# Residual and gate diagonal of the last units: from whole tiles on GpSimd to small pieces on ScalarE and VectorE

## The chip, the cores and the metric

The kernel runs on one core of one Trainium2 chip. The metric is the device time of one execution in microseconds, and the comparison is by the median of several runs. A core has a matrix engine (TensorE, PE in the profile), VectorE (DVE), ScalarE (ACT), GpSimd (POOL), and SyncE (SP), which here only issues transfers. Each engine works through its own list of instructions in the order of that list and waits for the others by semaphores.

## What is computed

One layer of a diffusion transformer on 256 tokens of 1024 channels: a token mixer, then a mixture of 64 experts (8 per token) with a shared expert, each followed by a residual sum and a LayerNorm. The change lies in the last part:

```python
x = layer_norm(alpha * x + g1 * y, ln1_g, ln1_b)
h = modulate(x, sh2, sc2)                      # normalise, scale, shift
scores = sigmoid(h @ w_router)                 # choose 8 of 64 experts per token, weights w
act = silu(einsum('td,edf->tef', h, w_e_gate)) * einsum('td,edf->tef', h, w_e_up) * gates
y2 = einsum('tef,efd->td', act, w_e_down) + shared(h)
x = layer_norm(alpha * x + g2 * y2, ln2_g, ln2_b)      # g2 from the conditioning vector
```

The change touches how `alpha * x` and the gate `g2` of the last line are prepared.

## The kernel before

The first 570 us (mixer, up to the first LayerNorm) are untouched. Then the experts are worked off in 29 units, 0 to 28. A unit is up to 128 gathered token rows of one to four experts. The weights of an expert come in two transfers of 1 MB for gate and up (`gu`) and one of 1 MB for down (`dn`), into a ring of six `gu` and seven `dn` buffers; SyncE issues each load as soon as the list in the source gives it a free buffer, and a load waits until the last matmul that reads the old content is done.

TensorE's order is written out by hand (`_program`, a list of steps, under `manual_schedule`). Per unit u: `g` gate and up (`gate_up`, line 1415, into PSUM `pgu`); `s` the first half of the scatter of unit u-1 (`scatter`, lines 1447 and 1448: matmuls into `py`, VectorE adds them to the sums `y`, which lie in `x1`); `P` the transposes of the next unit's weighted selection (`places`, `poh`, lines 1375 to 1379); `t` the activation (`act_t`: Silu on ScalarE at line 154, product with up on VectorE at line 1312, transposes `pat` on TensorE at line 1315, copy `at` on ScalarE at line 1317); `S` the second half of the scatter; on every other unit `G`, the gather of the next pair's rows (`gather`, 32 matmuls `pxg` at line 1391, evicted in turn by ScalarE, line 1394, and VectorE, line 1397); `d` the down product (line 1423), whose result is split into `rh` and `rl` (lines 1437 and 1438). `gated` (line 1365, VectorE) builds the weighted selection for the next unit. The order on ScalarE, VectorE and GpSimd comes from a scheduler that mostly follows the order of the source and the readiness of operands.

The residual of the last LayerNorm is kept as `x2h` + `x2l`, the normalised tokens in two parts, in an order of channels with k outer and p inner (channel 8p + k). `residual()` rebuilds alpha times the tokens from them, with `sd` = (alpha / rs, alpha * mu): for each of the two token tiles t, `end[:, t, :]` = (x2h + x2l) * sd0 + sd1, written to channel order, that is every eighth element for one k. It also writes `end[:, 3, :]`, the diagonal: the identity times the gate `mod2[:, 2, k]` for each k, 128x1024. `spread` (line 1534) turns this diagonal by a matmul with ones into the gate on all partitions, and ScalarE copies it into `end[:, 2, :]` (line 1535). `so_far` then multiplies the sums by the gate and adds them to the residual (lines 1542 and 1543).

`end` has no memory of its own: it takes a `gu` buffer, the first that is freed when no gate and up loads are left. That is after `gate_up` of unit 26, and the buffer is the one that held expert 5, the only expert of that unit. `spread` follows the down product of the same unit. Units 27 (experts 12 and 60) and 28 (experts 61 to 63) come after it, then `finish`, the LayerNorm and the output.

Of the kernel before, what the change touches and what calls it, by code (L numbers as in the profile page):

```python
# [9 lines left out]
F32 = mybir.dt.float32  # L10
# [3 lines left out]
AF = mybir.ActivationFunctionType  # L14
OP = mybir.AluOpType
AX = mybir.AxisListType

P = 128
D = 1024
T = 256  # L20
KD = 8
# [113 lines left out]
def build(ctx, tc, I, out, dbg=None):  # L135
    nc = tc.nc
# [31 lines left out]
    def C(name):  # L168
        a, b = _COLS[name]
        return cf[:, a:b] if b <= NKEEP else cm[:, a - NKEEP:b - NKEEP]  # L170

    ident = C("ident")
# [6 lines left out]
    mod2 = persist.tile([P, 3, KD], F32, name="mod2")  # L179
# [903 lines left out]
    for c, t, qs_ in ((0, 0, (0,)), (1, 0, (0,)), (0, 1, (0,)), (0, 0, (1,)), (1, 0, (1,)), (2, 0, (0, 1)),  # L1083
# [11 lines left out]
        if qs_[-1] == 0:  # L1095
# [4 lines left out]
                                       op0=OP.mult, op1=OP.add)  # L1100
# [43 lines left out]
    x2h = pkeep.tile([P, 2, KD, P], F32R, name="x2h")  # L1144
    x2l = pkeep.tile([P, 2, KD, P], F32R, name="x2l")
# [53 lines left out]
    for t in range(2):  # L1199
        ts = slice(t * P, (t + 1) * P)  # L1200
        for kk in (0, 4):
# [3 lines left out]
            for i in range(4):  # L1205
                k = kk + i
# [3 lines left out]
                else:  # L1210
                    on_act = nc.scalar.activation(h2[k][:, ts], pt[:, i * P:(i + 1) * P], AF.Identity,
                                                  bias=mod2[:, 0, k:k + 1], scale=mod2[:, 1, k:k + 1])
# [25 lines left out]
    for t in range(2):  # L1238
# [15 lines left out]
                                   op0=OP.add, op1=OP.mult)  # L1254
# [254 lines left out]
    def residual():  # L1509

        slot = free["g"].pop(0)
        end = ring[slot[0]].tile([P, 4, D], F32, tag=f"gu{slot[1]}", name="end", bufs=1)
        diag = end[:, 3, :].rearrange("q (k p) -> q k p", k=KD)
        nc.gpsimd.tensor_tensor(diag, ident[:, None, :].to_broadcast([P, KD, P]),
                                mod2[:, 2, :, None].to_broadcast([P, KD, P]), op=OP.mult)
        for t in range(2):
            mu, rs = stats2[t]
            sd = pkeep.tile([P, 2], F32, name=f"sd{t}")
            with tc.issue_after(last_rl[0]):
                nc.vector.reciprocal(sd[:, 0:1], rs)  # L1520
            nc.vector.tensor_scalar(sd[:, 0:1], sd[:, 0:1], ALPHA, None, op0=OP.mult)
            with tc.issue_after(last_rl[0]):
                nc.vector.tensor_scalar(sd[:, 1:2], mu, ALPHA, None, op0=OP.mult)
            e3 = end[:, t, :].rearrange("q (p k) -> q k p", k=KD)
            nc.gpsimd.tensor_tensor(e3, x2h[:, t].bitcast(F32), x2l[:, t].bitcast(F32), op=OP.add)
            nc.gpsimd.tensor_scalar(end[:, t, :], end[:, t, :], sd[:, 0:1], sd[:, 1:2], op0=OP.mult, op1=OP.add)
        return end

    def spread(end):
# [16 lines left out]
    end = None  # L1546
    assert steps[0] == ("g", 0)
    for op, i in steps[1:]:
# [8 lines left out]
        elif op == "g":  # L1557
            outs_[i] = gate_up(i)
            done("g", i)
            if end is None and free["g"] and not any(x == "g" for x, _ in loads):  # L1560
                assert i <= last_u - 2
                end, spread_at = residual(), i
        elif op == "t":
            _, used, gcol, _ = prep[i]
            ats_[i] = act_t(outs_.pop(i), gcol, used)
            if i == last_u - 1:
                so_far(end, 0)
        elif op == "d":
            if i == last_u:
                last_down(i, ats_.pop(i))  # L1570
            else:
                downs[i] = down(i, ats_.pop(i))
            if end is not None and i == spread_at:
                spread(end)
            done("d", i)
        else:
            n = "sS".index(op)
            (scatter_open if i == last_u - 1 else scatter)(n, *downs[i])
            if n and i == last_u - 2:
                so_far(end, 1)  # L1580
                xf, g2bc = end[:, 0:2, :], end[:, 2, :]
# [31 lines left out]
    with tc.If(nov > 0):  # L1613
# [3 lines left out]
        for k in range(KD):  # L1617
            px = ps_mm("px")
            for t in range(2):
                for part in (x2h, x2l):  # L1620
# [3 lines left out]
                                    op0=OP.mult, op1=OP.add)  # L1624
# [52 lines left out]
```

## Time and profile before

| | us |
|---|---|
| median of 3 runs (1095.12 to 1095.26) | 1095.15 |
| the profiled execution | 1096.06 |
| its span, first to last instruction | 1094.2 |
| TensorE busy | 1046.6 (96%) |
| VectorE busy | 636.2 (58%) |
| ScalarE busy | 424.1 (39%) |
| GpSimd busy | 91.1 (8%) |
| mean granted TensorE clock | 0.991 |

A busy TensorE is not TensorE at its peak: matmuls are pipelined, so that the durations of neighbours overlap, and the start of the next one tells more than the duration. [...] Timeline rows merge neighbours of one kind, and a bracket at a row's end is the engine's idle time before it and what ended it by the profile. Where an instruction waits for several semaphores, the one that came last is named, which can be a coincidence.

### The profile page before, as it was taken

The page shows a single profiled execution, that of the slowest core. Times are in us where ns is not written, and L with a number is a line of the kernel's source. Part 1 is how long each engine was busy: PE and PEld are TensorE (multiplying, and loading weights), DVE is VectorE, ACT ScalarE, POOL GpSimd, SP SyncE. Part 2 cuts the span into 40 slices and gives each one's busy share as a digit, 9 for nine tenths or more (in the row PEclk, how much of TensorE's full clock was granted, in tenths as well). Part 3 has the DMA queues.
Part 4 walks back from the last instruction along what each step waited for, and adds up shares of the span by engine and source line. Part 5 has one row for each costly group of instructions (what it writes and reads, how often), then busy time and mean ns, then how long its engine had stood idle before and what let it go on. Part 6 is the DMA issues. An engine that isn't in the chain of part 4 may idle for free.

```text
span 1094.2 us, 19256 instructions
## 1 busy us (share of the span) xinstructions
PE 1046.6 (96%) x7488; PEld 727.3 (66%) x7488; DVE 636.2 (58%) x1339; ACT 424.1 (39%) x779; POOL 91.1 (8%) x135
## 2 busy tenths in 40 slices
PE   4999999999999999999999899999999999999994
PEld 3797877979899988889997444445444444444441
DVE  5576584756854879778687334434433444444355
ACT  4573645646544767576424112122211221122120
POOL 1100000000132133210001000000000000000111
PEclk9999999999999999999998999999999999999998
DMA  9935533535686544524876879999999999999991
GB/s 319 322 117 168 178 110 125 191 97 174 190 202 155 129 93 93 102 81 127 308 289 271 364 275 417 425 422 424 423 426 425 424 420 415 421 409 397 426 402 43
DMA packets 115101, 295.38 MB, mean 270 GB/s; under 512 B 7080, under 2 KB 86896, under 8 KB 90432
## 3 DMA queue, kind: packets, MB, share of 16 engines
q1 hardware_dynamic: 113088, 290.46, 69.9%
q0 software_dynamic: 1776, 3.47, 3.7%
q8 instruction: 60, 0.98, 0.4%
q14 instruction: 33, 0.27, 0.1%
q10 hardware_dynamic: 144, 0.20, 0.0%
HBM read 293.05 MB, written 1.05 MB: 269 GB/s over the span
## 4 chain that ended last, share of the span: by engine, by line
PE 68%; DMA 10%; DVE 9%; issue 7%; ACT 3%; SPq 2%; POOL 1%; DVEq 0%; ACTq 0%; POOLq 0%
PE proj L388 20%; PE pgu L1415 13%; PE pdn L1423 6%; DMA dn<-in_w_e_down_dram 5%; PE proj L394 4%; PE pxg L1391 4%; DMA gu<-in_w_e_up_dram 3%; PE py L1447 2%; PE pv L394 2%; PE pa L461 2%; DVE wlo L336 1%; SPq L319 1%; PE pgu L1157 1%; PE o L394 1%; PE pu L779 1%
## 5 line engine op out<-in xcount | busy, mean ns | idle before, releaser
L1415 PE MATMUL pgu<-gu,xg 128*32 128x512 f32 (+2 forms) x1392 | 201.3, 593 | 2.1 <-DMA gu<-in_w_e_up_dram 1.9
L1415 PEld LDWEIGHTS pgu<-gu,xg 128*32 128x32 f32 (+2 forms) x1392 | 66.2, 117 | 133.7 <-issue 126.1
L336 DVE TENSOR_TENSOR wlo<-wraw,whi 128x1024 fp32r<-128x1024 f32 x102 | 126.1, 1238 | 47.3 <-ACT whi L335 45.2
L335 ACT CAST whi<-wraw 128x1024 fp32r<-128x1024 f32 x102 | 106.2, 1048 | 60.5 <-PE proj L388 45.8
L1312 DVE SCALAR_TENSOR_TENSOR ac<-ac,gcol,pgu 128x256 f32<-128x256 f32 (+1 forms) x28 | 13.4, 480 | 172.3 <-ACT ac L154 172.3
L1423 PE MATMUL pdn<-dn,at 128*32 128x512 f32 (+2 forms) x740 | 106.0, 589 | 0.0
L388 PE MATMUL proj<-hh,whi 128*128 128x256 f32 (+1 forms) x480 | 101.6, 329 | 0.0
L388 PE MATMUL proj<-hl,whi 128*128 128x256 f32 (+1 forms) x480 | 100.6, 323 | 0.0
L388 PE MATMUL proj<-hh,wlo 128*128 128x256 f32 (+1 forms) x480 | 97.4, 321 | 0.0
L154 ACT ACTIVATE ac<-pgu 128x256 f32<-128x256 f32 (+1 forms) x30 | 11.5, 384 | 179.0 <-PE pgu L1415 179.0
L388 PEld LDWEIGHTS proj<-hh,whi 128*128 128x128 f32 x480 | 72.5, 189 | 11.4 <-issue 4.2
L388 PEld LDWEIGHTS proj<-hh,wlo 128*128 128x128 f32 x480 | 73.9, 188 | 8.3 <-issue 1.4
L388 PEld LDWEIGHTS proj<-hl,whi 128*128 128x128 f32 x480 | 72.6, 189 | 6.2 <-issue 0.7
L1438 DVE TENSOR_TENSOR rl<-pdn,rh 128x512 fp32r<-128x512 f32 x56 | 38.6, 691 | 57.9 <-ACT rh L1437 57.8
L1437 ACT CAST rh<-pdn 128x512 fp32r<-128x512 f32 x56 | 32.8, 585 | 101.5 <-PE pdn L1423 92.2
L1448 DVE TENSOR_TENSOR x<-x,py 128x512 f32<-128x512 f32 x108 | 68.9, 678 | 0.0
L1423 PEld LDWEIGHTS pdn<-dn,at 128*32 128x32 f32 (+1 forms) x740 | 29.6, 116 | 57.8 <-issue 55.3
L1391 PE MATMUL pxg<-oh,x2h 128*128 128x256 f32 (+1 forms) x240 | 62.3, 297 | 2.0 <-DVE x L1448 1.5
L1391 PE MATMUL pxg<-oh,x2l 128*128 128x256 f32 (+1 forms) x240 | 59.7, 284 | 0.0
L1447 PE MATMUL py<-rh,ohs 128*128 128x512 f32 x108 | 50.0, 463 | 4.4 <-DVE x L1448 3.6
L1394 ACT ACTIVATE xg<-pxg,mod 128x256 f32<-128x256 f32 (+1 forms) x60 | 33.4, 557 | 45.3 <-PE pxg L1391 45.3
L1391 PEld LDWEIGHTS pxg<-oh,x2h 128*128 128x128 f32 x240 | 46.3, 193 | 5.9 <-DVE x L1448 3.0
(393 smaller groups left out, 1804.5 us busy)
## 6 DMA issues: line engine op xcount, KB each, us to landing
gu<-in_w_e_gate_dram SPq DMA_DIRECT2D x64, 1024.0 KB, 12.5
gu<-in_w_e_up_dram SPq DMA_DIRECT2D x64, 1024.0 KB, 13.9
dn<-in_w_e_down_dram SPq DMA_DIRECT2D x61, 1024.0 KB, 13.3
wraw<-in_w_in_dram SPq DMA_DIRECT2D x80, 512.0 KB, 5.1
wada<-in_w_ada_dram SPq DMA_DIRECT2D x48, 512.0 KB, 6.5
wraw<-in_w_branch_a_dram SPq DMA_DIRECT2D x8, 512.0 KB, 6.1
wraw<-in_w_branch_b_dram SPq DMA_DIRECT2D x8, 512.0 KB, 3.9
wraw<-in_w_out_dram SPq DMA_DIRECT2D x8, 512.0 KB, 9.4
```

The costliest lines, as they stand in the source:

```text
L335: nc.scalar.copy(hi, raw)
L336: nc.vector.tensor_sub(lo, raw, hi.bitcast(F32))
L388: nc.tensor.matmul(o, a[:, m * P:(m + 1) * P], b[:, :n], start=first, stop=last)
L394: nc.tensor.matmul(o, b[:, t * P:(t + 1) * P], a, start=first, stop=last)
L1391: nc.tensor.matmul(pg_, part[:, t, k, :], oh[:, t, :w_], start=(t == 0 and part is x2h), stop=(t == 1 and part is x2l))
L1394: nc.scalar.activation(xg[:, k, :w_], pg_, AF.Identity, bias=mod2[:, 0, k:k + 1], scale=mod2[:, 1, k:k + 1])
L1415: nc.tensor.matmul(o[s:s + w_], xg[:, k, i * P + s:i * P + s + w_], W["g"][j][:, :, k, :], start=(k == 0), stop=(k == KD - 1))
L1423: nc.tensor.matmul(pd[s:s + w_, :ns.stop - ns.start], at[:, jj, s:s + w_], W["d"][j][:, jj, ns], start=(jj == 0), stop=(jj == 1))
L1437: nc.scalar.copy(rh[:used], z)
L1438: last_rl[0] = nc.vector.tensor_sub(rl[:used], z, rh[:used].bitcast(F32)).ins
L1447: nc.tensor.matmul(py, ohs[:used, t * P:(t + 1) * P], a[:used], start=(q == 0), stop=(q == 1))
L1448: nc.vector.tensor_add(to[:, t, ns], to[:, t, ns], py)
```

## The change

In `residual()` the three kinds of GpSimd instruction go. The diagonal is made by eight activations on ScalarE (128x128 each, Identity with the gate's column as scale). Each token tile is made in four pieces of two k, that is 256 elements per partition: ScalarE writes x2h * sd0 + sd1 into the piece, then VectorE adds x2l * sd0 to it in place. The places that are written stay the same, and so does the buffer that `end` takes.

```diff
@@ -1511,8 +1511,8 @@
         slot = free["g"].pop(0)
         end = ring[slot[0]].tile([P, 4, D], F32, tag=f"gu{slot[1]}", name="end", bufs=1)
         diag = end[:, 3, :].rearrange("q (k p) -> q k p", k=KD)
-        nc.gpsimd.tensor_tensor(diag, ident[:, None, :].to_broadcast([P, KD, P]),
-                                mod2[:, 2, :, None].to_broadcast([P, KD, P]), op=OP.mult)
+        for k in range(KD):
+            nc.scalar.activation(diag[:, k, :], ident, AF.Identity, scale=mod2[:, 2, k:k + 1])
         for t in range(2):
             mu, rs = stats2[t]
             sd = pkeep.tile([P, 2], F32, name=f"sd{t}")
@@ -1522,8 +1522,12 @@
             with tc.issue_after(last_rl[0]):
                 nc.vector.tensor_scalar(sd[:, 1:2], mu, ALPHA, None, op0=OP.mult)
             e3 = end[:, t, :].rearrange("q (p k) -> q k p", k=KD)
-            nc.gpsimd.tensor_tensor(e3, x2h[:, t].bitcast(F32), x2l[:, t].bitcast(F32), op=OP.add)
-            nc.gpsimd.tensor_scalar(end[:, t, :], end[:, t, :], sd[:, 0:1], sd[:, 1:2], op0=OP.mult, op1=OP.add)
+            for k in range(0, KD, 2):
+                ks = slice(k, k + 2)
+                nc.scalar.activation(e3[:, ks], x2h[:, t, ks].bitcast(F32), AF.Identity, bias=sd[:, 1:2],
+                                     scale=sd[:, 0:1])
+                nc.vector.scalar_tensor_tensor(e3[:, ks], x2l[:, t, ks].bitcast(F32), sd[:, 0:1], e3[:, ks],
+                                               op0=OP.mult, op1=OP.add)
         return end
 
     def spread(end):
```

ScalarE's list around unit 26, the difference. `rh` before it belongs to unit 25's down product; `ac`, `at`, `xg`, the second `rh` and `end<-pg` belong to unit 26 and the gather behind it:

```order
 L1437 CAST rh<-pdn 128x512 x2
-L154 ACTIVATE ac<-pgu 128x256
-L1317 COPY at<-pat 128x256
-L1394 ACTIVATE xg<-pxg,mod_67 128x256 x4
-L1437 CAST rh<-pdn 128x512 x2
-L1535 COPY end<-pg_10727 128x4x128
-L1535 COPY end<-pg_10730 128x4x128
+L1515 ACTIVATE end<-cf,mod_67 128x128 x8
+L1527 ACTIVATE end<-x2h,sd_10625 128x2x128 x4
+L1527 ACTIVATE end<-x2h,sd_10637 128x2x128 x4
+L154 ACTIVATE ac<-pgu 128x256
+L1317 COPY at<-pat 128x256
```

The sixteen new activations stand directly ahead of unit 26's Silu; what followed Silu keeps its order.

VectorE's list at the same place, before, from behind the small column sums `sd` on (`x_66` is the tile of the sums y):

```order
L1521 TENSOR_SCALAR sd_10624<-sd_10624 128x1
L1312 SCALAR_TENSOR_TENSOR ac<-ac,gcol,pgu 128x256
L1448 TENSOR_TENSOR x_66<-x_66,py 128x512 x2
L1377 TENSOR_REDUCE gcol<-poh 128x1
L1379 TENSOR_SCALAR ohs<-poh 128x256
L1363 MEMSET ohg 128x2x32
L1365 TENSOR_TENSOR ohg<-oh,gj 128x2x96
L1448 TENSOR_TENSOR x_66<-x_66,py 128x512 x2
```

And in the changed kernel:

```order
L1521 TENSOR_SCALAR sd_10637<-sd_10637 128x1
L1448 TENSOR_TENSOR x_66<-x_66,py 128x512 x2
L1377 TENSOR_REDUCE gcol<-poh 128x1
L1379 TENSOR_SCALAR ohs<-poh 128x256
L1363 MEMSET ohg 128x2x32
L1365 TENSOR_TENSOR ohg<-oh,gj 128x2x96
L1529 SCALAR_TENSOR_TENSOR end<-x2l,sd_10625,end 128x2x128 x4
L1529 SCALAR_TENSOR_TENSOR end<-x2l,sd_10637,end 128x2x128 x4
L1312 SCALAR_TENSOR_TENSOR ac<-ac,gcol,pgu 128x256
L1448 TENSOR_TENSOR x_66<-x_66,py 128x512 x2
```

The product of Silu and up (line 1312) moved from the head of this piece to behind the first scatter sums, the gate's products (line 1365) and the eight new instructions. TensorE's list is the same in both kernels.

## Rows read from the trace of the kernel before

**Rows 1.** Busy time by stage; per engine us (count), then clock, DMA share, GB/s.

```profile
1036.00:1049.00 13.00, 11.26 (x57) 7.20 (x59) 8.53 (x15) 4.73 (x9) 8.51 (x5) 1.00 1.01 421
1049.00:1069.00 20.00, 19.92 (x156) 6.50 (x148) 10.84 (x19) 3.03 (x6) 0.00 (x0) 1.00 0.90 354
...
1068.00:1070.00 2.00, 2.00 (x13) 0.80 (x7) 0.24 (x1) 0.38 (x1) 0.00 (x0) 1.00 0.00 0
...
1069.00:1094.00 25.00, 10.72 (x61) 4.72 (x58) 13.99 (x28) 1.41 (x3) 3.81 (x3) 0.83 0.12 44
```

**Rows 2.** Timeline, TensorE, 1028 to 1049: start, us, engine, line, operation, tiles.

```profile
1028.03 7.13 PE L1415 MATMUL pgu<-gu,xg 128*128 128x512 f32 x16 [1.10 <-DMA gu<-in_w_e_up_dram]
...
1036.16 0.44 PE L1315 MATMUL pat<-cf,ac 128*128 128x128 f32 x2
1036.85 0.47 PE L1447 MATMUL py<-rh,ohs 128*128 128x512 f32 x1 [0.25 <-DVE x L1448]
...
1040.52 0.39 PE L1391 MATMUL pxg<-oh,x2h 128*128 128x256 f32 x1 [1.49 <-DVE x L1448]
...
1043.58 3.59 PE L1423 MATMUL pdn<-dn,at 128*128 128x512 f32 x8
1047.02 1.88 PE L1534 MATMUL pg<-end,ones 128*128 128x512 f32 x4
1048.83 1.49 PE L1415 MATMUL pgu<-gu,xg 128*32 128x512 f32 x12
```

**Rows 3.** Timeline of the same stretch, ScalarE, VectorE and GpSimd.

```profile
1035.20 0.39 ACT L154 ACTIVATE ac<-pgu 128x256 f32<-128x256 f32 x1 [7.54 <-PE pgu L1415]
...
1035.39 1.90 POOL L1514 TENSOR_TENSOR end<-cf,mod 128x1024 f32<-128x1024 f32 x1 [453.02 <-DMA dn<-in_w_e_down_dram]
...
1037.25 4.88 POOL L1525 TENSOR_TENSOR end<-x2h,x2l 128x1024 f32<-128x1024 f32 x2
...
1037.96 1.91 DVE L1365 TENSOR_TENSOR ohg<-oh,gj 128x192 f32<-128x192 f32 x1
...
1042.11 2.40 POOL L1526 TENSOR_SCALAR end<-end,sd 128x1024 f32<-128x1024 f32 x2
```

**Rows 4.** Groups by shape, VectorE, line 1365: count, busy us, mean ns, idle before.

```profile
L1365 DVE TENSOR_TENSOR ohg<-oh,gj 128x192 f32<-128x192 f32 x12 | 5.7, 478 | 0.0
```

**Rows 5.** Groups by shape, ScalarE, whole span.

```profile
L1011 ACT COPY PT<-pT 128x512 f32<-128x512 f32 x22 | 13.0, 590 | 1.5 <-PE pT L1010 1.2
...
L810 ACT ACTIVATE on<-po,ve 128x128 f32<-128x128 f32 x16 | 5.0, 365 | 4.9 <-POOL ve L808 4.9
...
L520 ACT ACTIVATE hf<-hf,mod 128x256 f32<-128x256 f32 x8 | 4.5, 596 | 7.0 <-DVE mod L512 7.0
...
L1535 ACT COPY end<-pg 128x512 f32<-128x512 f32 x2 | 2.0, 1124 | 0.3 <-PE pg L1534 0.3
```

**Rows 6.** Timeline, ScalarE, two pairs that run back to back, merged.

```profile
22.64 1.09 ACT L520 ACTIVATE hf<-hf,mod 128x256 f32<-128x256 f32 x2 [0.22 <-DVE mod L512]
...
108.41 0.62 ACT L810 ACTIVATE on<-po,ve 128x128 f32<-128x128 f32 x2 [0.72 <-POOL ve L808]
```

**Rows 7.** Groups by shape, VectorE, line 706.

```profile
L706 DVE SCALAR_TENSOR_TENSOR og<-og,vcol,sgq 128x256 f32<-128x256 f32 x8 | 3.8, 480 | 1.2 <-ACT sgq L154 1.2
```

**Rows 8.** A gap on TensorE's timeline, and two stretches of lower granted clock by windows.

```profile
576.51 1.83 PE L1204 MATMUL pt<-cf,x 128*128 128x128 f32 x8 [2.46 <-ACT x L1196]
...
576.50:577.00 0.50, 0.49 (x3) 0.49 (x4) 0.50 (x1) 0.50 (x1) 0.50 (x1) 0.70 0.94 393
...
583.00:583.50 0.50, 0.50 (x3) 0.41 (x2) 0.50 (x1) 0.00 (x0) 0.00 (x0) 0.50 1.01 426
583.50:584.00 0.50, 0.50 (x4) 0.45 (x3) 0.47 (x5) 0.35 (x1) 0.00 (x0) 0.98 0.93 393
...
627.50:628.00 0.50, 0.50 (x6) 0.50 (x6) 0.22 (x2) 0.00 (x0) 0.00 (x0) 0.90 0.82 344
...
631.00:631.50 0.50, 0.50 (x5) 0.50 (x5) 0.11 (x1) 0.08 (x1) 0.00 (x0) 0.69 0.00 0
```

## The prediction

> **What bounds the kernel now.** I read the table of busy time by stage first, because it shows which engine has no idle time left near the place that the change touches. From 1049 to 1069 us TensorE is busy for 19.92 of 20 us; from 1036 to 1049 it is busy for 11.26 of 13 [rows 1]. The weights stream until about 1068 us and then stop: in 1068 to 1070 the DMA share is 0.00 while TensorE is still fully busy, and after 1069 it is at 0.12 [rows 1]. So the last weights are in before the last units are computed, and from 1028 us on the end is set by TensorE's list and by the short hops to ScalarE and VectorE that TensorE waits for. Next I read the timeline of this stretch. Gate and up of unit 26 (expert 5, the last unit with a single expert) start at 1028.03, when their weights land, and run 7.13 us [rows 2]. That is the last DMA wait of over 1 us on TensorE. Behind it come the transposes of the activation (pat, 1036.16), the second half of unit 25's scatter (py, 1036.85), the last gather (pxg), unit 26's down product (1043.58), the spread of the gate's diagonal (1047.02) and unit 27 (1048.83) [rows 2]. Two gaps are visible: 0.25 us before py and 1.49 us before pxg, both ended by VectorE's line 1448 [rows 2].
>
> **The work that moves is off the path today.** GpSimd makes the diagonal and the two residual tiles in three kinds of instruction: 1.90, 4.88 and 2.40 us, 9.18 us in all, from 1035.39 to 1044.5 [rows 3]. Its first reader on TensorE is the spread at 1047.02 [rows 2], so it is done 2.5 us early and nobody waits for it. Taking it off GpSimd therefore gives nothing by itself. It could start no earlier either: GpSimd had been idle for 453 us and began at 1035.39 [rows 3], 0.23 us after unit 26's gate and up ended (1028.03 + 7.13 = 1035.16), because `end` is laid over the buffer of expert 5's gate and up weights. The row names a DMA as releaser, but among the waits is that on TensorE.
>
> **What is added on ScalarE, and where.** By the order of instructions the 16 new activations (8 of 128x128 for the diagonal, 8 of 128x256 for the residual) stand ahead of unit 26's Silu (line 154). They write `end`, so they wait for the same end of gate and up, 1035.16. Before, Silu starts at 1035.20, after 7.54 us of idle time [rows 3]: there is a hole ahead, but the buffer comes free only at its end. So all 16 pieces run first, and behind them are queued Silu, the copy of pat, and the four gather evictions. TensorE waits for Silu through line 1312 and pat.
>
> The price of a piece. Diagonal: 128x128 with a column as scale has its match in line 810, 0.365 us, two back to back in 0.62 [rows 5, 6], so each further one adds 0.62 - 0.365 = 0.255; it reads PSUM where the new one reads SBUF, and I take 0.28. 8 x 0.28 = 2.2 us. Residual: 128x256 from SBUF with scale and bias columns is line 520, 0.596 us, two in 1.09, so 0.49 each [rows 5, 6]. But the new ones write every eighth element. The copy of line 1535 also writes so and takes 1.124 us for 512 elements, where line 1011's plain copy of the same size takes 0.590 [rows 5]: 0.534 more, or 0.27 for 256. So 0.49 + 0.27 = 0.76, and 8 x 0.76 = 6.1 us. Sum **8.3 us**. Bounds: if the spaced write costs nothing, 2.2 + 8 x 0.49 = 6.1; if nothing overlaps, 8 x 0.4 + 8 x 0.86 = 10.1. I take the middle because rows of this kernel show both the overlap and the price of the spaced write. No other table of functions is loaded there, in the order as built.
>
> **What is added on VectorE.** Eight 128x256 scalar_tensor_tensor follow the ScalarE pieces one by one, and line 1312 stands behind them. Line 706, the same kind from SBUF, takes 0.48 us [rows 7], less than the 0.76 of a ScalarE piece, so seven are hidden under ScalarE and only the last counts; Silu (0.39) runs beside that one. Compared with today's hop of 0.96 us from Silu's start to pat (1035.20 to 1036.16), the last piece's end and this instruction add about 0.2. VectorE is not blocked meanwhile: unit 25's first scatter sums, line 1377 and the gate's products (line 1365) now stand ahead of the eight. Delay of pat: 8.3 + 0.2 = **8.5 us**.
>
> **What is given back.** Line 1365 took 1.91 us at 1037.96, beside GpSimd's two-input add that began at 1037.25 [rows 3]. The 12 of that shape are busy for 5.7 us together [rows 4], so the other 11 take (5.7 - 1.9) / 11 = 0.35. The 1.56 us more are VectorE waiting for GpSimd; line 1448 came late, and TensorE waited 1.49 us at pxg. [...] With GpSimd empty and line 1365 done during ScalarE's pieces, both gaps go: **-1.7 us** (1.49 + 0.25). At worst only the larger, -1.5.
>
> **The new idle stretch and TensorE's clock.** TensorE's list does not change. So from 1036.2, where pat starts today, it has nothing until 1036.16 + 8.5 = 1044.7: over 8 us. [...] What follows (py, 32 pxg, pdn) is dense, so half of the slow time is lost: 1.7 or 3.4 us, and I take **+2.4**. [...] Without the loss the sum would be 6.8 us instead of 9.2.
>
> **The sum.** 8.5 - 1.7 + 2.4 = **+9.2 us**. None of it is won back later, since TensorE has 0.08 us of idle time from 1049 to 1069, and the transfers, already over at 1068, do not wait for ScalarE. All loads of gate and up weights are queued by then, and the buffers of the last down weights are freed by unit 25, ahead of the change. On the profiled execution, 1096.06 (its span 1094.2 and 1.9 around it), that gives 1105.3; it lies 0.9 above the median of the runs, 1095.15, to which the forecast refers: **1104.4 us**.
>
> **Rivals.** (a) *Faster.* The pieces fill ScalarE's hole before Silu: 8.3 us of pieces against 7.54 of idle time [rows 3]. Then Silu is late by under 1 us, nothing idles long, and the 1.7 come back: 1095.15 + 0.8 + 0.2 - 1.7 = 1094.5, and 1093.5 with pieces at their cheap bound. It decides by when the buffer is free. Against it: GpSimd, idle and first in its own queue, could not start before 1035.39. [...] Chance 0.04.
> (b) *No change.* The tail hides the delay, because something else ends last: this needs weights that land some 9 us after TensorE wants them. The DMA share of 0.00 from 1068 [rows 1] speaks against it. 1095.2, chance 0.03.
> (c) *The clock does not fall, or is back at once.* +6.8: 1102.0. For it: after the 1.49 us gap at 1040.52 nothing of the kind is seen. Against it, the length of the new gap. Chance 0.10.
> (d) *VectorE sets the pace.* If spaced reading and writing doubles its piece to 0.96 us, the chain is 2.2 + 0.76 + 8 x 0.96 = 10.6 instead of 8.3 + 0.48, so +1.9: 1106.3. For it, the doubled copy of line 1535, though that is ScalarE. Chance 0.11.
>
> **How the numbers follow.** Forecast 0.72, (a) 0.04, (b) 0.03, (c) 0.10, (d) 0.11. The forecast's own ends: cheap pieces and the short slow stretch, 6.1 + 0.2 - 1.7 + 1.7 = +6.3, 1101.5; dear pieces and the long one, 10.1 + 0.2 - 1.5 + 3.4 = +12.2, 1107.3. Cheap pieces without a clock loss would give +4.6, 1099.7. The range is 1099.5 to 1107.2: it takes in (c) and (d), and leaves out (a), (b) and the dearest corner. What can be told from no change is about 0.2%, 2.2 us: faster 0.04, same 0.03, slower 0.93.
>
> **What would show it.** In the changed profile ScalarE should begin the diagonal at about 1035.2, the last residual piece should end near 1043.6 and Silu start there; each spaced piece should add 0.76 us. TensorE should show one idle stretch of about 8 us before pat, ended by line 1312, then matmuls at a granted clock of 0.50 for 3 to 7 us. Line 1365 should take 0.35 us and the gap before pxg be gone. Gate and up of unit 27 should start some 9 us later than 1048.83, and everything after should keep its distances. Pieces that start before 1035 would prove me wrong in the direction of (a); a later stage that shortens, in the direction of (b).

## The result, and the profile after

The changed kernel takes 1102.1 us (median of 4 runs, 1101.0 to 1103.0) beside 1095.13 for the kernel before: +7.0 us, a ratio of 1.0059 with a 95% interval of 1.0047 to 1.0072. The forecast was 1104.4 with a range of 1099.5 to 1107.2. The direction and the mechanism came as forecast; the loss is 2.3 us smaller.

The profiled execution of the changed kernel took 1100.99 us (span 1099.2). Its difference from the profiled execution of before, 4.9 us, is not the effect of the change alone, because gate and up of unit 26 already start 2.2 us sooner in it. The stretch of granted clock 0.50 (1.00 is full speed) from 627.9 to 631.3 in before [rows 8] is missing here, which is most of it: a pxg starts 0.214 us after the one ahead of it in that stretch and 0.118 behind the stretch, so some 1.5 of the 3.4 us. It lies ahead of the first instruction that the change touches. I therefore measure all kernels below between two marks in the same trace, the starts of gate and up of unit 26 and of unit 27. Before, the distance is 1048.83 - 1028.03 = 20.80 us [rows 2].

TensorE's timeline of the changed kernel over that stretch (start, us, engine, line, operation, tiles, and in brackets the idle time ahead and what ended it), the counterpart of [rows 2]:

```profile
1025.82 7.13 PE L1415 MATMUL pgu<-gu,xg 128*128 128x512 f32 x16 [0.96 <-DMA gu<-in_w_e_up_dram]
...
1041.58 0.69 PE L1315 MATMUL pat<-cf,ac 128*128 128x128 f32 x2 [7.48 <-DVE ac L1312]
1041.92 0.78 PE L1447 MATMUL py<-rh,ohs 128*128 128x512 f32 x1
...
1043.78 0.41 PE L1391 MATMUL pxg<-oh,x2h 128*128 128x256 f32 x1
...
1048.12 3.59 PE L1423 MATMUL pdn<-dn,at 128*128 128x512 f32 x8
...
1053.37 7.07 PE L1415 MATMUL pgu<-gu,xg 128*32 128x512 f32 x64
```

From unit 26 to unit 27 it is now 1053.37 - 1025.82 = 27.55 us, 6.75 more. One idle stretch of 7.48 us stands ahead of pat, ended by line 1312, and the two gaps before py and pxg of [rows 2] are gone. The distance splits in three: start to pat 15.76 us (before 8.13, so +7.63), pat to pdn 6.54 (before 7.42, so -0.88), pdn to unit 27 5.25 in both.

ScalarE and VectorE in the same stretch, same columns, the counterpart of [rows 3]:

```profile
1033.04 2.45 ACT L1515 ACTIVATE end<-cf,mod 128x128 f32<-128x128 f32 x8 [7.45 <-PE pgu L1415]
1035.39 5.04 ACT L1527 ACTIVATE end<-x2h,sd 128x256 f32<-128x256 f32 x8
1040.23 0.41 ACT L154 ACTIVATE ac<-pgu 128x256 f32<-128x256 f32 x1
...
1035.40 0.29 DVE L1365 TENSOR_TENSOR ohg<-oh,gj 128x192 f32<-128x192 f32 x1
1036.26 4.88 DVE L1529 SCALAR_TENSOR_TENSOR end<-x2l,sd,end 128x256 f32<-128x256 f32 x8 [0.57 <-ACT end L1527]
1041.06 0.47 DVE L1312 SCALAR_TENSOR_TENSOR ac<-ac,gcol,pgu 128x256 f32<-128x256 f32 x1
```

ScalarE is idle for 7.45 us and then starts the pieces only 0.09 us after gate and up end (1025.82 + 7.13 = 1032.95): the hole is there, and the pieces cannot use it. Silu (line 154) follows 7.19 us behind the first piece. Line 1365 takes 0.29 us in place of 1.91.

The new instructions one by one, in the view of single lines (duration in ns as minimum/median/maximum, then the first and last start):

```profile
L1515 ACT ACTIVATE end<-cf,mod x8: 386/387/402, 1033.0 to 1035.1; 128x128 f32<-128x128 f32 x8
...
L1527 ACT ACTIVATE end<-x2h,sd x8: 798/800/830, 1035.4 to 1039.6; 128x256 f32<-128x256 f32 x8
...
L1529 DVE SCALAR_TENSOR_TENSOR end<-x2l,sd,end x8: 679/681/689, 1036.3 to 1040.5; 128x256 f32<-128x256 f32 x8
```

A piece of the diagonal takes 0.387 us and is followed by the next after (2.45 - 0.387) / 7 = 0.295; a piece of the residual takes 0.800 and is followed after (5.04 - 0.80) / 7 = 0.605.

Last the windows of the changed kernel (stretch; its length; busy us and count of PE, PEld, DVE, ACT, POOL; granted clock; DMA share; GB/s), the counterpart of [rows 1] and, for the clock, of [rows 8]:

```profile
1038.00:1038.50 0.50, 0.00 (x0) 0.00 (x0) 0.50 (x2) 0.50 (x3) 0.00 (x0) 0.71 1.11 459
1038.50:1039.00 0.50, 0.00 (x0) 0.00 (x0) 0.50 (x2) 0.50 (x2) 0.00 (x0) 0.50 0.95 393
...
1044.50:1045.00 0.50, 0.50 (x4) 0.50 (x4) 0.21 (x1) 0.13 (x1) 0.00 (x0) 0.50 1.16 492
1045.00:1045.50 0.50, 0.50 (x6) 0.50 (x5) 0.01 (x1) 0.44 (x1) 0.00 (x0) 0.96 0.85 360
...
1053.00:1073.00 20.00, 19.91 (x155) 6.66 (x156) 10.97 (x20) 3.58 (x6) 0.00 (x0) 1.00 0.58 221
1072.00:1074.00 2.00, 2.00 (x16) 0.55 (x11) 0.00 (x0) 0.11 (x1) 0.00 (x0) 1.00 0.00 0
```

The clock falls to 0.50 at 1038.2 (0.71 is 0.50 for the last 0.29 of that half microsecond) while TensorE has nothing to do, and is back at 1045.0. TensorE resumes at 1041.58, so 3.4 us of the slow stretch held work. From unit 27 on TensorE is as full as before (19.91 of 20 us), the weights end ahead of it (DMA share 0.00 from 1072), and everything keeps its distance. The last row of VectorE's timeline, before and then in the changed kernel:

```profile
1088.94 1.00 DVE L204 SCALAR_TENSOR_TENSOR xo<-xo,rs,bc 128x512 f32<-128x512 f32 x2
...
1093.47 1.00 DVE L204 SCALAR_TENSOR_TENSOR xo<-xo,rs,bc 128x512 f32<-128x512 f32 x2
```

It moved by 4.53 us, and unit 27, from 1048.83 to 1053.37, by 4.54. The rest of the span's 5.0 lies behind that last row: 5.3 us from its start to the end of the span before, 5.7 after. Of the kernels below, the one that leaves all this work on GpSimd (GpSimd's adds later) has 5.2 us there, and the others have 5.6 to 5.7. So moving any of the work went with 0.3 to 0.5 us at the very end; what sets it is open.

### The profile page after: what moved, and what is told of

The parts are those of the page before. It is cut to its first block, busy times and chain, and to the rows that moved or that the text cites. A ratio compares the mean times of both kernels' runs of the same rounds, so it can differ in the third digit from the quotient of the medians.

```text
span 1099.2 us, 19267 instructions
## 1 busy us (share of the span) xinstructions
PE 1044.6 (95%) x7488; PEld 723.2 (66%) x7488; DVE 639.8 (58%) x1347; ACT 431.5 (39%) x795; POOL 81.4 (7%) x130
## 3 DMA queue, kind: packets, MB, share of 16 engines
HBM read 293.05 MB, written 1.05 MB: 268 GB/s over the span
## 4 chain that ended last, share of the span: by engine, by line
PE 72%; DVE 10%; DMA 8%; ACT 4%; issue 3%; SPq 3%; POOL 0%; DVEq 0%; ACTq 0%; POOLq 0%
PE proj L388 20%; PE pgu L1415 15%; PE pdn L1423 7%; DMA gu<-in_w_e_up_dram 6%; PE pxg L1391 5%; PE proj L394 4%; PE py L1447 3%; PE pv L394 2%; DMA dn<-in_w_e_down_dram 2%; PE pa L461 2%; DVE wlo L336 1%; SPq L319 1%; PE pgu L1157 1%; PE o L394 1%; DVE x L1448 1%
## 5 line engine op out<-in xcount | busy, mean ns | idle before, releaser
L1415 PEld LDWEIGHTS pgu<-gu,xg 128*32 128x32 f32 (+2 forms) x1392 | 63.2, 117 | 135.8 <-issue 132.9
L189 POOL TENSOR_TENSOR rs<-ve,nhalf 128x1 f32<-128x1 f32 (+1 forms) x9 | 7.5, 834 | 584.5 <-DVE ve L187 584.4
```

The costliest lines, as they stand in the source:

```text
L1415: nc.tensor.matmul(o[s:s + w_], xg[:, k, i * P + s:i * P + s + w_], W["g"][j][:, :, k, :], start=(k == 0), stop=(k == KD - 1))
```

## The experiments

The theory to be tested, called the queue theory below: the pieces cost because they stand ahead of unit 26's Silu on ScalarE's queue and can start no sooner than Silu could; the empty GpSimd gives some 2 us back at line 1365; the idle stretch costs some 1.4 to 2.4 us through the slow clock. Its rivals: the clock theory (most of the loss is the clock); that the pieces cost wherever they stand; that the gap before pxg was not GpSimd's doing. In the last two columns stand the distances between the two marks, and from unit 26 to pat, each from one trace.

| kernel | median, us (range; runs) | ratio to before, 95% interval | unit 26 to 27, us | 26 to pat, us |
|---|---|---|---|---|
| before | 1095.13 (1094.83 to 1095.26; 4) | | 20.80 | 8.13 |
| changed | 1102.1 (1101.0 to 1103.0; 4) | 1.0059 (1.0047 to 1.0072) | 27.55 | 15.76 |
| clock held up | 1100.05 (1099.6 to 1103.4; 5) | 1.0055 (1.0034 to 1.0076) | 26.26 | 16.03 |
| diagonal alone | 1096.3 (1094.7 to 1099.2; 10) | 1.0011 (1.0000 to 1.0022) | 20.75 | 10.51 |
| residual alone | 1101.9 (1100.5 to 1107.2; 5) | 1.0074 (1.0048 to 1.0101) | 27.48 | 15.84 |
| pieces later | 1094.08 (1093.5 to 1095.9; 10) | 0.9990 (0.9980 to 0.9999) | 19.18 | 8.13 |
| pieces later, again | 1093.98 (1092.2 to 1095.7; 12) | 0.9983 (0.9975 to 0.9992) | 19.17 | 8.13 |
| GpSimd's adds later | 1093.39 (1092.4 to 1095.1; 12) | 0.9980 (0.9972 to 0.9989) | 19.20 | 8.13 |
| neighbouring elements | 1102.52 (1) | | 27.10 | 14.58 |

The kernels from the third to the sixth row ran beside runs of before with a median of 1095.13 (1093.7 to 1097.4; 21), the last three beside 1095.67 (1093.9 to 1097.7; 23). That spread is wider than in the first comparison, which is why the two marks carry the argument.

**The clock held up.** The changed kernel, with 30 matmuls whose results nobody reads between unit 25's last matmul and pat, so that TensorE hardly idles there (0.93 us is left ahead of pat).

```diff
+            if i == last_u - 2:
+                warm = ps_dn()
+                for n in range(30):
+                    nc.tensor.matmul(warm, x2h[:, 0, 0, :], x2h[:, 0, 0:4, :], start=True, stop=True)
```

> The changed kernel with 30 extra matmuls (128x512, results unused) between poh and pat, so that TensorE is busy for most of the 7.5 us in which it has nothing to do. Queue theory (the sixteen pieces ahead of Silu are the cost; the slower clock adds a smaller share): pat still waits for line 1312, but the granted clock stays at 1.00, so py and the first pxg run at full pace; the run keeps its 7.0 us over before less the clock's share of 1.4 to 2.4: 1099.7 to 1100.7. Clock theory (most of the cost is the slow clock behind the idle stretch): below 1098.5. If the clock costs nothing here: 1102.1 as the changed kernel. The spread of the single runs, 2 us in the changed kernel, should shrink if it comes from the length of the slow stretch.

TensorE's timeline of this kernel, and below it the window of this stretch in the same columns as above:

```profile
1034.12 7.07 PE L1572 MATMUL pdn<-x2h 128*128 128x512 f32 x30
1042.12 0.44 PE L1315 MATMUL pat<-cf,ac 128*128 128x128 f32 x2 [0.93 <-DVE ac L1312]
1042.31 0.48 PE L1447 MATMUL py<-rh,ohs 128*128 128x512 f32 x1
...
1043.32 0.28 PE L1391 MATMUL pxg<-oh,x2h 128*128 128x256 f32 x1
...
1047.10 3.60 PE L1423 MATMUL pdn<-dn,at 128*128 128x512 f32 x8
...
1052.35 7.07 PE L1415 MATMUL pgu<-gu,xg 128*32 128x512 f32 x64
```

```profile
1034.00:1047.00 13.00, 12.07 (x71) 10.37 (x70) 10.37 (x20) 9.36 (x21) 0.00 (x0) 1.00 1.01 423
```

The clock stays at 1.00, and pat to pdn falls from 6.54 to 4.98 us: the slow clock costs 1.56 us there. Against before (7.42) the stretch is now 2.44 us shorter; that is what was given back. The whole distance gains only 1.29, because pat comes 0.27 later (a piece of line 1527 takes 0.85 instead of 0.80 us beside these matmuls, the eight 5.23 instead of 5.04). 5.46 us of the 6.75 remain with the clock at full speed, so the clock theory falls. The median, 1100.05, lies where the queue theory put it. The spread of the single runs, which should have shrunk if it came from the slow stretch, did not: 3.8 us over five runs, beside 2.0 over four of the changed kernel.

**The diagonal alone.** The kernel before, with only the eight activations of the diagonal moved to ScalarE.

```diff
-        nc.gpsimd.tensor_tensor(diag, ident[:, None, :].to_broadcast([P, KD, P]),
-                                mod2[:, 2, :, None].to_broadcast([P, KD, P]), op=OP.mult)
+        for k in range(KD):
+            nc.scalar.activation(diag[:, k, :], ident, AF.Identity, scale=mod2[:, 2, k:k + 1])
```

> The kernel before with the diagonal alone moved to eight pieces on ScalarE; the residual stays on GpSimd. Queue theory: eight pieces of 0.29 delay Silu by 2.35 us and pat by about 2.5; line 1365 comes at about 1037.6 beside the first GpSimd add, waits 0.3 us at most and the gap of 1.49 us and that of 0.25 go; with no fall of the clock 1095.1 + 2.5 - 2.2 = 1095.4, with one up to 1.4 us more, 1096.8. Clock theory: 2.2 us or less over before only if the clock falls. If the mere presence of pieces on ScalarE costs nothing: 1093.5.

Its timeline, TensorE, GpSimd and VectorE:

```profile
1037.59 0.44 PE L1315 MATMUL pat<-cf,ac 128*128 128x128 f32 x2 [2.22 <-DVE ac L1312]
...
1042.58 3.60 PE L1423 MATMUL pdn<-dn,at 128*128 128x512 f32 x8
...
1034.44 4.88 POOL L1525 TENSOR_TENSOR end<-x2h,x2l 128x1024 f32<-128x1024 f32 x2 [452.46 <-DMA dn<-in_w_e_down_dram]
...
1036.65 0.39 DVE L1365 TENSOR_TENSOR ohg<-oh,gj 128x192 f32<-128x192 f32 x1
```

Pat comes 2.38 us later, and pat to pdn takes 4.99 instead of 7.42: lost and won are equal, and the distance is 20.75 against 20.80. Between the marks that is a delay that costs nothing, by cancellation and not because it is hidden. It is won because VectorE does its scatter sums and line 1365 while TensorE waits for pat, and line 1365 is hardly held up: GpSimd's first add now runs from 1034.44 to some 1036.9 (half of 4.88 us), and line 1365 comes at 1036.65, as it ends. An idle stretch of 2.2 us did not bring the clock down here: it is 1.00 from 1027 to 1050. Without a fall of the clock I had expected 1095.4; the median, 1096.3, is 0.9 above that and 1.2 above before. Some 0.5 us of this is what lies behind VectorE's last row; the rest no row shows, and the interval of the ratio begins at 1.0000.

**The residual alone.** The changed kernel with the diagonal put back on GpSimd (the diff above, reversed).

> The kernel before with the residual alone moved to pieces on ScalarE and VectorE; the diagonal stays on GpSimd. Queue theory: eight pieces of 0.605 are 4.85 us ahead of Silu; here VectorE's list puts line 1377, 1379 and 1365 behind the pieces and ahead of line 1312, some 1.3 us more; pat is late by about 6.5, the two gaps (2.2) go, the clock falls and takes 1.4: about +5.7, 1100.8. Without a fall of the clock 1099.4. Clock theory: as the changed kernel, 1102, since the idle stretch is long in both.

Its timeline, ScalarE, VectorE and TensorE:

```profile
1033.68 5.07 ACT L1527 ACTIVATE end<-x2h,sd 128x256 f32<-128x256 f32 x8 [7.40 <-PE pgu L1415]
1038.56 0.41 ACT L154 ACTIVATE ac<-pgu 128x256 f32<-128x256 f32 x1
...
1034.70 3.85 DVE L1529 SCALAR_TENSOR_TENSOR end<-x2l,sd,end 128x256 f32<-128x256 f32 x5
1038.46 0.68 DVE L1448 TENSOR_TENSOR x<-x,py 128x512 f32<-128x512 f32 x1
1039.06 1.85 DVE L1529 SCALAR_TENSOR_TENSOR end<-x2l,sd,end 128x256 f32<-128x256 f32 x3
...
1041.78 0.47 DVE L1312 SCALAR_TENSOR_TENSOR ac<-ac,gcol,pgu 128x256 f32<-128x256 f32 x1
...
1042.30 0.69 PE L1315 MATMUL pat<-cf,ac 128*128 128x128 f32 x2 [7.56 <-DVE ac L1312]
```

Its GpSimd, and the view of single lines for VectorE's pieces:

```profile
1033.82 1.90 POOL L1514 TENSOR_TENSOR end<-cf,mod 128x1024 f32<-128x1024 f32 x1 [451.81 <-DMA dn<-in_w_e_down_dram]
...
L1529 DVE SCALAR_TENSOR_TENSOR end<-x2l,sd,end x8: 672/674/1491, 1034.7 to 1040.2; 128x256 f32<-128x256 f32 x8
```

ScalarE is 2.3 us less late with Silu than in the changed kernel, as it should be, and yet pat is as late (15.84 against 15.76 us). I had allowed 1.3 us for lines 1377, 1379 and 1365 behind VectorE's pieces and expected pat 6.5 us later than before; it is 7.71 later. With the diagonal gone from ScalarE, five of VectorE's pieces move ahead of one of unit 25's scatter sums (line 1448) too, so VectorE is the last, and Silu's result waits from 1038.97 (1038.56 + 0.41) to 1041.78. One of the pieces also took 1.49 us instead of 0.67, beside GpSimd's diagonal. The median of 1101.9 is 1.1 above what I expected, and it is the 1102 that the clock theory had for this kernel. The rows do not bear that theory out: pat waits for line 1312, and from pat to pdn this kernel takes 6.39 us, no more than the changed one (6.54). So this run does not price the residual on ScalarE; it shows VectorE's queue as the bound, the outcome of rival (d), in a neighbour of the changed kernel, though by the order of its list and not by slower pieces. The last three pieces, which have nothing left to wait for, follow one another after (1.85 - 0.67) / 2 = 0.59 us.

**The pieces later.** The diagonal on GpSimd as before, the same pieces of the residual (eight on ScalarE, eight on VectorE) behind the evictions of the gate's diagonal (line 1535 of the kernel before), where ScalarE waits for unit 27; `behind` is the last of these evictions, which `spread` now returns.

```diff
+                with tc.issue_after(behind):
+                    nc.scalar.activation(e3[:, ks], x2h[:, t, ks].bitcast(F32), AF.Identity, bias=sd[:, 1:2],
+                                         scale=sd[:, 0:1])
...
-                spread(end)
+                pieces_of_residual(end, spread(end))
```

> The same residual pieces on ScalarE and VectorE as in the changed kernel, but placed behind the spread's copies, in the 5.9 us that ScalarE has no work during unit 27's gate and up; the diagonal stays whole on GpSimd. Queue theory (place, not kind): 8 x 0.605 = 4.8 us fit into the hole, Silu of unit 26 is not delayed, GpSimd runs no two-input add beside line 1365, so the gaps of 1.49 and 0.25 us go and nothing is added: 1093.4 to 1093.6. Rival (the small pieces cost wherever they stand): over 1096. Rival (the gap before pxg is not GpSimd's doing): 1095.1.

Its timeline, ScalarE and TensorE:

```profile
1045.53 2.02 ACT L1543 COPY end<-pg 128x512 f32<-128x512 f32 x2 [0.27 <-PE pg L1542]
1047.34 5.10 ACT L1532 ACTIVATE end<-x2h,sd 128x256 f32<-128x256 f32 x8
1053.45 0.38 ACT L154 ACTIVATE ac<-pgu 128x256 f32<-128x256 f32 x1 [1.01 <-PE pgu L1415]
...
1035.24 0.44 PE L1315 MATMUL pat<-cf,ac 128*128 128x128 f32 x2
1035.93 0.47 PE L1447 MATMUL py<-rh,ohs 128*128 128x512 f32 x1 [0.25 <-DVE x L1448]
...
1037.00 0.28 PE L1391 MATMUL pxg<-oh,x2h 128*128 128x256 f32 x1
...
1041.04 3.60 PE L1423 MATMUL pdn<-dn,at 128*128 128x512 f32 x8
...
1046.29 7.07 PE L1415 MATMUL pgu<-gu,xg 128*32 128x512 f32 x64
```

The residual's activations, 5.10 us here, stand in a hole of which 1.01 us is left behind them, when the next Silu waits for TensorE. Pat is where it was (8.13), pat to pdn takes 5.80 instead of 7.42, and the distance falls to 19.18. Of the two gaps only the one before pxg is gone; the 0.25 us before py, which I had also counted, stays. The pieces do not cost wherever they stand. The median, 1094.08, is 1.05 under before, where I had expected some 1.6; between the marks 1.62 are won, and some 0.4 more stand behind VectorE's last row. It ran a second time:

> The diagonal on GpSimd as before, the sixteen pieces of the residual behind the evictions of the gate's diagonal, where ScalarE and VectorE wait for unit 27. Repeats the earlier kernel of this form beside the one that only holds the GpSimd adds back. Queue theory: both lose the gap before pxg and nothing else, so they agree within 0.3 us, unit 26 to 27 19.2 us, some 1093.5. Rival: the pieces cost something of their own where VectorE's eight stand beside unit 27 (line 154 of unit 27 later), then this one is slower than the other by 0.5 us or more.

The distance is 19.17 us again, and the median is 1.7 us under the runs of before beside it.

**GpSimd's adds later.** The kernel before with all work left on GpSimd; only the two adds wait, through a VectorE memset of one column of `end`, until line 1365 (`behind`) is done.

```diff
+            with tc.issue_after(behind):
+                nc.vector.memset(end[:, t, 0:1], 0.0)
             nc.gpsimd.tensor_tensor(e3, x2h[:, t].bitcast(F32), x2l[:, t].bitcast(F32), op=OP.add)
```

> Residual and diagonal stay on GpSimd as before; only the two-input adds are held back until VectorE has made the gate's products of line 1365 (a VectorE memset of one column of end behind that line, which the add must wait for). If the gap of 1.49 us before pxg comes only from GpSimd's add standing beside line 1365 (1.91 instead of 0.35 us), line 1365 takes 0.3 to 0.4 us, the gap is gone and unit 27 starts 1.5 to 1.6 us sooner after unit 26 than before: 19.2 to 19.3 us instead of 20.80, some 1093.5 in time. Rival: the gap belongs to something else that the late pieces moved too, then unit 27 keeps its 20.8 us and the time stays at 1095.1.

Its timeline, VectorE, GpSimd and TensorE; line 1365 of the others is line 1367 here:

```profile
1036.06 0.29 DVE L1367 TENSOR_TENSOR ohg<-oh,gj 128x192 f32<-128x192 f32 x1
...
1036.46 4.77 POOL L1534 TENSOR_TENSOR end<-x2h,x2l 128x1024 f32<-128x1024 f32 x2 [1.06 <-DVE end L1533]
...
1045.33 7.07 PE L1418 MATMUL pgu<-gu,xg 128*32 128x512 f32 x64
```

19.20 us, the same as with the pieces later. The medians of the two lie 0.6 us apart, within their spread but more than the 0.5 that I had put to the rival, that the late pieces cost something of their own. The sign I had named for it is missing: unit 27's Silu starts 7.17 us after unit 27 in both, and VectorE's last row 40.13. Some 0.4 us of the difference lies behind that row, where the cause is open. So what was to be had at this place was not the instructions on GpSimd but where two of them stood in time, and no engine had to be changed for it. This kernel is 2.3 us (0.2%) under the runs of before beside it, and so, like the one with the pieces later, ahead of both kernels of the case.

**Neighbouring elements.** The changed kernel, each residual piece written as 256 neighbouring elements instead of every eighth, which puts the residual's channels in another order. It ran once, and only its rows are used.

```diff
-            e3 = end[:, t, :].rearrange("q (p k) -> q k p", k=KD)
+            e3 = end[:, t, :].rearrange("q (k p) -> q k p", k=KD)
```

> The changed kernel with each piece of the residual written as 256 neighbouring elements instead of every eighth, so its output has the channels of the residual in another order (this part of the computation is not the reference's). It prices the spaced write. If that write costs the 0.27 us of the prediction, an activation of line 1527 falls from 0.80 to 0.53 us and the eight from 5.04 to some 2.9 to 3.9, and pat comes 1.2 to 2.1 us sooner than in the changed kernel; if the price is the 0.20 us between line 1527 (0.80) and line 520 (0.596), the duration falls to 0.60 and the eight take about 4.0. Should VectorE's piece (0.68 us) fall to the 0.48 of line 706, its spaced read and write cost 0.20. Rival: neither falls, then the price lies in something else than the spacing of the writes, since the reading side stays as it is.

The views of single lines, TensorE's timeline, and the windows of the clock, in this kernel:

```profile
L1527 ACT ACTIVATE end<-x2h,sd x8: 584/584/586, 1037.3 to 1040.8; 128x256 f32<-128x256 f32 x8
...
L1529 DVE SCALAR_TENSOR_TENSOR end<-x2l,sd,end x8: 484/484/486, 1038.0 to 1041.4; 128x256 f32<-128x256 f32 x8
```

```profile
1042.34 0.69 PE L1315 MATMUL pat<-cf,ac 128*128 128x128 f32 x2 [6.30 <-DVE ac L1312]
...
1049.61 3.60 PE L1423 MATMUL pdn<-dn,at 128*128 128x512 f32 x8
```

```profile
1040.50:1041.00 0.50, 0.00 (x0) 0.00 (x0) 0.49 (x2) 0.50 (x2) 0.00 (x0) 0.60 1.06 442
...
1047.00:1047.50 0.50, 0.50 (x5) 0.50 (x4) 0.02 (x1) 0.17 (x1) 0.00 (x0) 0.58 1.13 475
```

A piece on ScalarE falls from 0.800 to 0.584 us and the eight from 5.04 to 4.03, so the next follows after (4.03 - 0.584) / 7 = 0.492 (its pitch: the time from one start to the next); VectorE's falls from 0.681 to 0.484, that of [rows 7]. Of the prices expected, 0.20 was near and 0.27 too high. The spacing costs 0.22 us of duration but only 0.605 - 0.492 = 0.11 per piece in a row, because spaced pieces overlap by 0.195 us and neighbouring ones by 0.092. Pat comes 1.18 us sooner (14.58 against 15.76), and only 0.45 of that arrives at unit 27: here the clock is at 0.50 from 1040.6 to 1047.4, so 5.1 us of it hold work, and pat to pdn takes 7.27 us instead of 6.54.

## Why the prediction was right, and where its sizes were off

Between the two marks the forecast was +9.2 us and the measured value is +6.75. The time alone would not have told the forecast from its rival (c): without a fall of the clock the sum was 1102.0, nearer to the measured 1102.1 than the forecast's 1104.4. The rows decide it. By the forecast's own terms:

| term | predicted | measured | from |
|---|---|---|---|
| sixteen pieces ahead of Silu | 8.3 | 7.2 | 1033.04 to 1040.23 |
| last VectorE piece and hop | +0.2 | +0.4 | Silu to pat 1.35 against 0.96 |
| given back | -1.7 | -2.4 | pat to pdn 4.98 (clock held up) against 7.42 |
| slow clock | +2.4 | +1.6 | pat to pdn 6.54 against 4.98 |
| sum | +9.2 | +6.8 | 27.55 against 20.80 |

The first two terms stand against 8.5 us in the prediction and are 7.6 together, the 7.63 by which pat is late.

- **Where the pieces start, and who waits.** Right. `end` is free only when gate and up are over, so the 7.45 us hole ahead of Silu helps nobody; rival (a) fell with the first ScalarE row. That the diagonal alone, ahead of Silu, delays pat by 2.38 us, and that the residual's eight activations delay Silu by their whole length there (1035.39 to 1040.23) and nothing behind the evictions, shows that the place in the queue is what costs.
- **The price of a residual piece.** The diagonal was right (0.295 a piece against 0.28). The residual was put at 0.76 and measured 0.605, 8 x 0.155 = 1.2 us in all. The larger part of that comes from adding the spaced write's 0.27 to a pitch: 0.49 was the time from one piece to the next, 0.27 a difference of durations. The pitch of neighbouring elements was right (0.492 measured); the spacing adds 0.22 to a duration and half of that to a pitch. So 0.05 of the 0.155 is the price itself, taken from copies, and 0.10 the sum of unlike times.
- **VectorE's piece.** Put at 0.48, measured 0.68, since it reads and writes spaced elements too (0.484 with neighbouring elements). The eight still follow ScalarE's pace ((4.88 - 0.68) / 7 = 0.60 us from one to the next), so only the last one shows, in the hop from Silu to pat (0.4 for 0.2), and rival (d) did not come about. It was near: where VectorE has nothing to wait for, in the run with the residual alone, its pieces follow after 0.59 us, hardly less than ScalarE's 0.605.
- **What is given back.** That GpSimd's add beside line 1365 was what held it up is shown: with the adds merely held back until line 1365 is done, line 1365 takes 0.29 us and 1.6 us come back. The term counted two idle gaps, 1.74 us, and left out that TensorE, once it has been held up elsewhere, finds everything behind pat ready: pat to py is 0.19 us in the run with the clock held up and 0.69 before and with the pieces later, and pxg to pdn 3.78 against 4.04 with the pieces later. With 0.06 in between that is the other 0.8 us, of which the prediction had counted the gap of 0.25 before py, and it exists only because of the delay.
- **The clock.** That it falls was right, and after the stretch TensorE did resume at 0.50 (pat at 1041.58, back at full clock at 1045.0). No run shows the 2.4 us that the sum has for it; the runs show 1.56 in its place (pat to pdn 6.54 against 4.98 with the clock held up). The 2.4 was my estimate, taken between half of the 3.4 us of the later slow stretch in [rows 8] and half of the 6.8 of the earlier one (576.7 to 583.5). Its size was off because I took the length of an earlier slow stretch as time that holds work. Here it began 3.4 us before TensorE resumed, so half was spent idle.
- **Nothing is won back later.** Right, to 0.01 us (4.53 and 4.54 us), so rival (b) falls; rival (c) falls because the clock did fall.

Three of the four size errors had the same sign, so they added up instead of cancelling.

## What to carry to other kernels

An engine's low busy share is no room for work if the work becomes free at the same moment as the instruction that everyone waits for: ask when the operands or the buffer come free, and what stands behind the new instructions in that queue. Before moving work off a slow engine, see whether anybody waits for its result; here nobody did, and the harm it did (1.6 us, one instruction of another engine held up) went away by starting that GpSimd work 1.1 us later. When pricing instructions in a row, add pitches to pitches and durations to durations, and measure effects of some microseconds between two marks inside a trace, since the parts ahead of the change differ by as much from one execution to the next: gate and up of unit 26 started at 1028.03 in one profile here and at 1025.82 in the other.

## What was not expected of the hardware

- How long GpSimd's add held up line 1365 depended on when that came, and in both runs that show it the delay ended with the add that was running, not when GpSimd was idle: with adds of 2.44 us, line 1365 took 1.91 us when it came 0.7 us into one [rows 3], and 0.39 when it came 0.2 us before one ended. In line with that, one of VectorE's pieces took 1.49 us instead of 0.67 beside GpSimd's diagonal. Line 1448, with one of its two inputs in PSUM, was not held up: it ran beside the second add of before, at 1039.79, in 1.27 us for two, the same as with the pieces later, where GpSimd has no add.
- The clock fell inside the idle stretch, not at its end: at 1038.2 with no work since 1034.1 in the changed kernel, at 1040.6 with none since 1036.0 with neighbouring elements, and it was still slow for 3.4 and 5.1 us of work afterwards. A shorter delay therefore met more of the slow stretch: 1.18 us won on ScalarE gave 0.45 at the end. After the 2.2 us idle stretch of the diagonal alone it did not fall.
- ScalarE's activations in a row overlap by 0.195 us when they write every eighth element, and by 0.092 when they write neighbours, so the spacing is cheaper in a row than the duration tells.
